# One dense column in four parts, tied between the four stages of the seam's inverse

## The chip, the cores and the metric

The kernel runs on one core of a Trainium2 chip. The metric is the device time of one execution in microseconds (us), as the median of several runs. It was 3087.81 us before the change (three runs, 3085.42 to 3102.24).

## The reference

Two layers act on 528 tokens (16 meta tokens and 512 others) of width 1024, in float32. Each layer is a half-step SwiGLU feed-forward block, a mixer, and a second feed-forward block, each closed by a layer norm. The mixer is what the change touches:

```python
def _mixer(x, w_in, ...):
    z = x @ w_in                                   # 1024 -> 7424 columns
    glu_a, glu_b, zr, gate_c, gate_r = split(z)
    yc = conv_branch(glu_a * sigmoid(glu_b))       # 31 taps per channel, layer norm, silu, matmul
    yr = rwkv_branch(zr)                           # 16 heads of 64; S is 64x64 for each head
    h = sigmoid(gate_c) * yc + sigmoid(gate_r) * yr
    return h @ w_out
...
def step(S, inp):                                  # the scan in rwkv_branch, token by token
    sa = einsum("bhvk,bhk->bhv", S, -kk_t)
    S = S * w_t + sa * (kk_t * a_t) + v_t * k_t
    return S, einsum("bhvk,bhk->bhv", S, r_t)
```

## The kernel before

Matrix products with weights are done in three float32r products (high by high, high by low part of the tokens, low by high part). A *dense column* is 128 columns of `w_in`: eight tiles of the inner dimension, three products each, in two halves of 264 tokens, 48 products in all (`mac`, L243). Its weights come by one transfer on SP's queue (`wunit`, L136), are split on ACT (`w_hi`, L145 or L147) and on DVE (`w_lo`, L158; for the gate columns 42 to 57 by an ACT copy and a subtracting transfer on POOL's queue, L151 and L152), and the sum is taken from PSUM by ACT or DVE. Two buffers each are there for the raw weights, for the split weights, and for the PSUM tile `mm` of a column.

The token-by-token scan is done in eight chunks of 64 tokens, for four groups `q` of four heads, one after the other. For each group:

- `prep` makes the decayed keys and queries from six dense columns (k, r and v for two pairs of heads).
- `scores` makes a first part for the meta tokens, and then for each chunk transposes (L1227) and score matrices (L1236). All of them use the one PSUM tile `sc`; ACT (L1229, L1241) and DVE (L1243, L1245) empty it before the next chunk may start. The triangular blocks go out to DRAM (`mscr`).
- `substitution` reads 16x16 blocks back (`im`), inverts them by 15 pairs of DVE steps (L1271, L1274), and brings the result through DRAM (`xdscr`) to the block diagonal `dd` by 16 transfers on SP's queue (L1285).
- `inverse` extends that to 64x64 blocks in four stages: 16 products (L1310), a masking by DVE (L1311), and three times 16 products (L1317) and an addition by DVE (L1318). ACT copies the result to `G`. It runs for two halves of the chunks: half 0 ahead of the scan, half 1 inside it.
- `meta` handles the meta tokens (L1336 to L1348 and `pairs`, L1426), and `scan` does the eight chunks: transposes (L1381), L1386, L1395 and L1398, L1403, with copies by ACT and updates of the state by DVE (L1409, L1410) between them.

The scan of group q carries the scores of group q+1 in its chunks. The *seam* is what stands in the program between two scans: the second substitution, the inverse of half 0 and `meta`. There are four inverses of half 0 in each layer: one ahead of the first scan and three at the seams between scans.

The remaining dense columns, for the convolution's input (`glu_b`, `glu_a`) and the gates (`gate`), are *fill*: a list from which `filler(n)` takes the next n. FILL0, FILL, FILLS and FILLP say how many are taken at which place. The convolution's 31 taps per block of channels are DVE work at low priority (L1065).

The order on each engine is not the program's order: a scheduler places instructions by priority (the place in the program, shifted by `high_priority`) as soon as its own estimates have their inputs and buffers ready. So it moves dense products of later columns up into places where PE would wait. Tiles of a pool take their buffers in the program's order. `nosync(later, earlier)` binds two instructions to an order and has no wait on the chip, where both are on one engine.

Of the kernel before, what the change touches and what calls it, by code (L numbers as in the profile page):

```python
# [10 lines left out]
AF = mybir.ActivationFunctionType  # L11
# [7 lines left out]
KT = D // P  # L19
SEQ = 512  # L20
NM = 16
T = NM + SEQ
# [46 lines left out]
TMP = 2  # L69


FILL0 = (0, 0, 0, 0, 2, 0, 0, 0, 2)
FILL = ((0, 0, 0, 0, 0, 0, 0, 0), (0, 0, 0, 0, 0, 0, 0, 0), (0, 0, 0, 0, 0, 0, 0, 0), (0, 1, 0, 1, 0, 1, 0, 0))
FILLS = (3, 3, 4, 2)
FILLP = ((0, 0, 0, 0, 0, 0), (0, 0, 0, 0, 0, 2), (0, 0, 0, 0, 0, 1), (0, 0, 0, 0, 0, 0))
LAST = 1
SCORES = (2, 1, 1, 1, 1, 1, 1, 1)
# [19 lines left out]
class Trunk:  # L97
# [72 lines left out]
    def stream(self, jobs, tail=0, before=None, ahead=None, between=None):  # L170


        def run(js):
            ws = [load() for load, mac, evac in js]
            if js is end and ahead is not None and AEARLY:
                ahead()
            for h in range(2):
                if h == 1 and js is end and between is not None:
                    if ahead is not None and not AEARLY:
                        ahead()  # L180
                    between()
                for w, (load, mac, evac) in zip(ws, js):
                    ps, products = mac(w, h)
                    self.together(products[:1])
                    self.together(products[1:])
                    evac(h, ps)

        end = jobs[len(jobs) - tail:]
        for job in jobs[:len(jobs) - tail]:
            run([job])  # L190
        if before is not None:
            before()
        run(end)
# [40 lines left out]
    def mac(self, pm, w, x, t0, n, nk, wk=0, xk=0, first=True, last=True):  # L234

        hi, lo = w
        xh, xl = x
        nc = self.nc
        for k in range(nk):
            for j, (a, b) in enumerate(((hi, xh), (hi, xl), (lo, xh))):  # L240
                for h in range(2):
                    s = t0 + h * n
                    m = self.issued = nc.tensor.matmul(  # L243
                        pm[:, h, :n], a[:, wk + k, :], b[:, xk + k, s:s + n],
                        start=first and k == 0 and j == 0,
                        stop=last and k == nk - 1 and j == 2)
                    if self.later is not None:
                        self.nosync(m, self.later)
                        self.later = None


    def setup(self):
# [199 lines left out]
    def ffn(self, l, which, t0, n, gname, bname, pre, final=False, head=None, extra=()):  # L452
# [197 lines left out]
        for f in range(m):  # L650
            gate(f, 0, ps[f], zs[f])
        for f, x in enumerate(heads(1)):
            gate(f, 1, x, zs[f])
# [115 lines left out]
    def mixer(self, l, last, pre, more):  # L769
        nc, tc = self.nc, self.tc  # L770
# [16 lines left out]
        first = [[pm[:, h, :T // 2] for h in range(2)] for pm in pms + [self.glu0]]  # L787
# [24 lines left out]
            self.cu.append(u)  # L812
        fill = []
        for ct in range(KT):
            fill += [lambda ct=ct: self.glu_b(ct), lambda ct=ct: self.glu_a(ct)]
        fill += [lambda o=o: self.gate(o) for o in range(2 * KT)]

        def filler(n):
            for _ in range(min(n, len(fill))):
                fill.pop(0)()  # L820

        self.mixer_begin(pms, filler)

        def prep(q):
            Q = {}
            for i, _ in enumerate(self.prep(q, Q)):
                filler(FILLP[q][i])
                self.taps(TAPP[q])
            return Q

        Q = prep(0)
        for c, _ in enumerate(self.scores(0, Q)):
            if c == 4:
                self.substitution(0, 0, Q)
            filler(FILL0[c])
            if c:
                self.taps(TAP0[2])
        self.substitution(0, 1, Q)
        self.inverse(0, 0, Q)
        self.meta(0, Q)  # L840
        N = prep(1)
        post = iter(())
        self.cuts = CUTS
        for q in range(4):
            scores = self.scores(q + 1, N) if q < 3 else iter(())
            early = None
            done = 0
            for c, _ in enumerate(self.scan(q, Q)):
                if c == 0:
                    self.inverse(q, 1, Q)  # L850
                with self.tc.high_priority(offset=-SC_LATE):
                    for _ in range(SCORES[c]):
                        next(scores, None)
                        done += 1
                        if done == 5 and q < 3:
                            self.substitution(q + 1, 0, N)
                if c >= POST:
                    next(post, None)
                if q == 3 and c >= G3:
                    if early is None:  # L860
                        early = self.post(q, Q)
                    with self.tc.high_priority(offset=-G3L):
                        next(early) if c < G3 + 5 else None
                filler(FILL[q][c])
                self.taps(TAP[q][c])
            for _ in post:
                pass
            if q < 3:
                self.substitution(q + 1, 1, N)
                self.inverse(q + 1, 0, N)  # L870
                self.meta(q + 1, N)
            post = early or self.post(q, Q)
            filler(FILLS[q])
            Q, N = N, prep(q + 2) if q < 2 else None
# [45 lines left out]
    def proj(self, col):  # L920
        w = self.loaded.pop(col) if col in self.loaded else self.load_in(col)
        pm = self.mm()
        self.mac(pm, w, self.x, 0, T // 2, KT)
        return pm

    def tv(self, x):
        return self.halves(x, 0, T // 2)
# [97 lines left out]
        nc.gpsimd.memset(self.dd, 0.0)  # L1025


    def glu_b(self, ct):
        self.glu_s = self.tmp("glus", 1)
        gv = self.tv(self.glu_s)  # L1030
        if ct == 0:
            self.nc.scalar.activation(gv, self.pv(self.glu0), AF.Tanh, scale=0.5)
        else:
            self.nc.scalar.activation(gv, self.pv(self.proj(8 + ct)), AF.Tanh, scale=0.5)

    def glu_a(self, ct):
        nc = self.nc
        pa = self.proj(ct)
        nc.vector.scalar_tensor_tensor(self.tv(self.glu_s), self.tv(self.glu_s), 1.0, self.pv(pa),
                                       op0=ALU.add, op1=ALU.mult)  # L1040
        nc.sync.dma_start(out=self.us[ct * P:(ct + 1) * P, :], in_=self.glu_s)
        self.convs.append(self.conv(ct))
# [27 lines left out]
                nc.sync.dma_start(out=self.cs[ct * P:(ct + 1) * P, a:], in_=acc[:, a:])  # L1070
            yield True

    def gate(self, o):

        pg = self.proj(50 + o if o < KT else 42 + o - KT)
        s = self.tmp("glus", 1)
        self.nc.scalar.activation(self.tv(s), self.pv(pg), AF.Tanh, scale=0.5)
        a = self.t0
        (self.nc.sync, self.nc.scalar, self.nc.gpsimd)[GQ].dma_start(out=self.gs[o * P:(o + 1) * P, a:], in_=s[:, a:])
# [211 lines left out]
            nc.sync.dma_start(out=xt0, in_=self.xs0[q].rearrange("s i t -> i s t"))  # L1291
            Q["xt0"] = xt0

    def inverse(self, q, g, Q):

        nc, mp = self.nc, self.mp
        N = NCH
        k = slice(g * N, (g + 1) * N)  # L1300
        U, d, dt = self.ut[:, k], self.dd[:, k, 0], self.dd[:, k, 1]
        t = mp.tile([P, NCH * 4, 32], F32, name="b4", bufs=B4).rearrange("p a b -> p (a b)")
        vt, y = (t[:, i * N * C:(i + 1) * N * C].rearrange("p (s i) -> p s i", i=C)
                 for i in range(2))
        ps = self.sc()[:, 0].rearrange("p (s t) -> p s t", t=C)

        halves = [slice(0, C), slice(C, P)]
        for i in range(N):
            for r in halves:
                nc.tensor.matmul(ps[r, i], U[r, i], d[r, i], start=True, stop=True)  # L1310
        nc.vector.tensor_tensor(vt, ps, self.mskb[:, None, :].to_broadcast([P, N, C]), op=ALU.mult)  # L1311
        x = dt
        for c0 in (0, 2 * NM, 2 * NM):
            cs = slice(c0, C)
            for i in range(N):
                for r in halves:
                    nc.tensor.matmul(ps[r, i, cs], vt[r, i], x[r, i, cs], start=True, stop=True)  # L1317
            nc.vector.tensor_tensor(y[:, :, cs], ps[:, :, cs], dt[:, :, cs], op=ALU.add)  # L1318
            x = y
        out = Q["G"].rearrange("a p e f t -> a (p e) f t")  # L1320
        out = out[0:C, :, 1, NM + g * 4 * C:NM + (g + 1) * 4 * C].rearrange(
            "a h (k e t) -> a k e h t", e=2, t=C)
        for e, r in enumerate(halves):
            nc.scalar.copy(out[:, :, e], y[r].rearrange("a (k h) t -> a k h t", h=4))


    def new_state(self):
# [400 lines left out]
```

## Time and profile before

| | |
|---|---|
| median of three runs | 3087.81 us |
| profiled execution | 3091.81 us |
| its span, first to last instruction | 3090.1 us |
| PE busy | 3007.7 us (97%) |
| DVE busy | 2278.4 us (74%) |
| ACT busy | 1435.9 us (46%) |
| mean granted TensorE clock | 0.981 |

The span lies within the execution's own time. Busy times of PE are modelled ends of pipelined matmuls. A row of the windows view has the window in us from the span's start, its length, the busy time and the count of instructions of each engine, the granted clock, the share of the DMA engines and GB/s; a mean clock of 0.82 is a mixture of stretches at 1.00 and at 0.50. A row of the timeline has start, duration, engine, line, operation, tiles, shape, count, and in brackets the idle time ahead and what ended it.

### The profile page before, as it was taken

How to read it: one execution, taken by the hardware profiler on the slowest of the kernel's cores; microseconds unless marked ns; L12 is line 12 of the kernel's file. 1: busy time of each engine (PE TensorE's matmuls, PEld its weight loads, DVE VectorE, ACT ScalarE, POOL GpSimd, SP SyncE). 2: the span in 40 equal slices, each digit the busy share in tenths (PEclk: the TensorE clock that was granted, in tenths of full speed). 3: DMA queues.
4: the chain of work that ended last, by engine and by line, in shares of the span. 5: the costliest groups of instructions: out<-in, count | busy, mean ns of one | idle time of the engine just before them, and what ended most of it. 6: DMA issues, size and time to landing. Idle time of an engine off the chain costs nothing.

```text
span 3090.1 us, 64229 instructions
## 1 busy us (share of the span) xinstructions
PE 3007.7 (97%) x26138; PEld 2883.1 (93%) x26138; DVE 2278.4 (74%) x4687; ACT 1435.9 (46%) x2551; POOL 178.5 (6%) x286
## 2 busy tenths in 40 slices
PE   8999999999999999999999999999999999999998
PEld 8999989888888899999999999899889889999998
DVE  5676777888886668666786768778788857677767
ACT  4454454344454444444454444543445545254443
POOL 0010000000000000010001000000000000001100
PEclk9999999899999999999999999999899999999999
DMA  6565534335355554565545654444254655546661
GB/s 180 144 148 130 127 116 150 94 90 136 95 135 137 170 145 123 135 148 142 127 128 127 151 130 120 136 134 105 73 137 111 151 131 167 154 121 146 151 145 57
DMA packets 555701, 405.29 MB, mean 131 GB/s; under 512 B 89292, under 2 KB 500288, under 8 KB 555406
## 3 DMA queue, kind: packets, MB, share of 16 engines
q1 hardware_dynamic: 519854, 308.49, 34.8%
q0 software_dynamic: 30944, 84.18, 14.8%
q10 hardware_dynamic: 4608, 8.52, 0.8%
q8 instruction: 205, 3.36, 0.5%
q14 instruction: 90, 0.74, 0.1%
HBM read 270.81 MB, written 47.12 MB: 103 GB/s over the span
## 4 chain that ended last, share of the span: by engine, by line
PE 80%; DVE 8%; DMA 5%; ACT 4%; issue 2%; SPq 1%; ACTq 0%; POOL 0%; DVEq 0%; POOLq 0%
PE mm L215 51%; PE mm L243 15%; PE ch L1403 2%; PE sc L1317 2%; PE tr L1386 1%; PE sc L1236 1%; PE ch L1395 1%; DMA w_raw<-in_w_in_dram 1%; DVE w_lo L158 1%; DVE cacc L1065 1%; DMA w_raw<-in_ffn_wu_dram 1%; ACT w_hi L147 1%; PE sc L989 1%; DVE ln_rstd L425 1%; DMA w_lo<-w_raw 1%
## 5 line engine op out<-in xcount | busy, mean ns | idle before, releaser
L215 PE MATMUL mm<-xh,w_hi 128*128 128x264 f32 (+1 forms) x1792 | 512.2, 287 | 11.3 <-ACT xh L441 5.9
L215 PE MATMUL mm<-xl,w_hi 128*128 128x264 f32 (+1 forms) x1792 | 511.1, 286 | 0.7 <-DVE xl L442 0.3
L215 PE MATMUL mm<-xh,w_lo 128*128 128x264 f32 (+1 forms) x1792 | 510.1, 285 | 0.5 <-DVE w_lo L158 0.5
L215 PE MATMUL mm<-hh,w_hi 128*128 128x264 f32 (+1 forms) x1408 | 399.3, 284 | 1.1 <-ACT hh L110 1.1
L215 PE MATMUL mm<-hl,w_hi 128*128 128x264 f32 (+1 forms) x1408 | 399.4, 284 | 0.5 <-DVE hl L111 0.4
L215 PE MATMUL mm<-hh,w_lo 128*128 128x264 f32 (+1 forms) x1408 | 399.6, 284 | 0.0
L243 PE MATMUL mm<-xh,w_lo 128*128 128x264 f32 x1760 | 387.9, 297 | 7.2 <-DMA w_lo<-w_raw 6.7
L243 PE MATMUL mm<-xh,w_hi 128*128 128x264 f32 x1760 | 384.0, 295 | 6.9 <-DVE kp L939 2.9
L243 PE MATMUL mm<-xl,w_hi 128*128 128x264 f32 x1760 | 383.6, 295 | 0.0
L1065 DVE SCALAR_TENSOR_TENSOR cacc<-cu,cw,cacc 128x528 f32<-128x528 f32 (+1 forms) x480 | 355.6, 752 | 4.2 <-ACT cacc L1063 0.4
L215 PEld LDWEIGHTS mm<-xh,w_hi 128*128 128x128 f32 x1792 | 339.3, 190 | 15.4 <-ACT xh L441 8.5
L215 PEld LDWEIGHTS mm<-xl,w_hi 128*128 128x128 f32 x1792 | 341.2, 190 | 2.4 <-DVE xl L442 2.3
L215 PEld LDWEIGHTS mm<-xh,w_lo 128*128 128x128 f32 x1792 | 340.9, 190 | 0.8 <-DVE w_lo L158 0.8
L120 ACT CAST w_hi<-sums 128x512 fp32r<-128x512 f32 (+1 forms) x204 | 154.7, 759 | 317.1 <-PE mm L215 205.4
L243 PEld LDWEIGHTS mm<-xh,w_lo 128*128 128x128 f32 x1760 | 283.2, 193 | 14.8 <-DMA w_lo<-w_raw 7.8
L243 PEld LDWEIGHTS mm<-xh,w_hi 128*128 128x128 f32 x1760 | 282.5, 193 | 13.4 <-DVE kp L939 3.2
L243 PEld LDWEIGHTS mm<-xl,w_hi 128*128 128x128 f32 x1760 | 282.1, 192 | 5.5
L215 PEld LDWEIGHTS mm<-hh,w_hi 128*128 128x128 f32 x1408 | 264.6, 188 | 1.8 <-ACT hh L110 1.5
L215 PEld LDWEIGHTS mm<-hl,w_hi 128*128 128x128 f32 x1408 | 264.9, 188 | 1.2 <-DVE hl L111 1.1
L215 PEld LDWEIGHTS mm<-hh,w_lo 128*128 128x128 f32 x1408 | 265.5, 189 | 0.1
L158 DVE TENSOR_TENSOR w_lo<-w_raw,w_hi 128x1024 fp32r<-128x1024 f32 (+1 forms) x192 | 204.0, 1064 | 74.7 <-ACT w_hi L147 68.3
L147 ACT CAST w_hi<-w_raw 128x1024 fp32r<-128x1024 f32 x136 | 142.4, 1049 | 249.8 <-PE mm L243 77.7
(362 smaller groups left out, 6838.4 us busy)
## 6 DMA issues: line engine op xcount, KB each, us to landing
w_raw<-in_w_in_dram SPq DMA_DIRECT2D x116, 512.0 KB
w_lo<-w_raw POOLq DMA_DIRECT2D x100, 512.0 KB, 5.0
w_raw<-in_ffn_wg_dram SPq DMA_DIRECT2D x88, 512.0 KB
w_raw<-in_ffn_wu_dram SPq DMA_DIRECT2D x88, 512.0 KB
w_raw<-in_ffn_wd_dram SPq DMA_DIRECT2D x80, 512.0 KB
w_lo<-w_raw POOLq DMA_DIRECT2D x68, 256.0 KB, 3.4
w_raw<-in_rwkv_wo_dram SPq DMA_DIRECT2D x16, 512.0 KB
w_raw<-in_conv_wo_dram SPq DMA_DIRECT2D x16, 512.0 KB
```

The lines of the kernel that those rows point to most:

```text
L120: self.nc.scalar.copy(hi, x)
L147: copy = self.nc.scalar.copy(hi[:, :kt], raw[:, :kt])
L158: sub = self.nc.vector.tensor_tensor(lo[:, k], raw[:, k], hi[:, k].bitcast(F32), op=ALU.subtract)
L215: self.issued = self.nc.tensor.matmul(pm, a[:, k, :], b[:, xk + k, s], start=first and k == 0 and j == 0, stop=last and k == nk - 1 and j ...
L243: m = self.issued = nc.tensor.matmul(pm[:, h, :n], a[:, wk + k, :], b[:, xk + k, s:s + n], start=first and k == 0 and j == 0, stop=last an ...
L425: nc.vector.reciprocal(rstd[:, :n], rstd[:, :n])
L989: nc.tensor.matmul(pm, w[a][r, o, :], x[b][r, s], start=j == 0, stop=j == 2)
L1065: tap = nc.vector.scalar_tensor_tensor(y, x, w, y, op0=ALU.mult, op1=ALU.add)
L1236: pairs.append(nc.tensor.matmul(ps[:, e, p * P:(p + 1) * P], FB[p][r, fs], G[r, p, 1, :, cs], start=True, stop=True))
L1317: nc.tensor.matmul(ps[r, i, cs], vt[r, i], x[r, i, cs], start=True, stop=True)
L1386: nc.tensor.matmul(tr[0:C, right(h)], G[:, h // 2, h % 2, 0, cs], sv[:, h, :], start=True, stop=True)
L1403: chain.append(nc.tensor.matmul(ch[rows, right(h)], SB[:, c, h, rows], va[:, h, :], start=False, stop=True, skip_group_check=True))
```

## The change

At each inverse of half 0 the next fill column is taken, its 48 products are cut in four parts of 12 (two tiles of the inner dimension), and one part is issued behind each of the four stages. `between` binds a part's first product behind the stage's last one, and the next stage's first product is bound behind the part's last (`after`; after the fourth part nothing is bound). The column's eviction (`column[1]`) follows the inverse. FILL0's last entry and three of the four entries of FILLS give up one column each, so each layer has the same columns as before. `glu_b`, `glu_a` and `gate` now get the PSUM tile handed in.

```diff
-FILL0 = (0, 0, 0, 0, 2, 0, 0, 0, 2)
+FILL0 = (0, 0, 0, 0, 2, 0, 0, 0, 1)
...
-FILLS = (3, 3, 4, 2)
+FILLS = (2, 2, 3, 2)
...
-        self.inverse(0, 0, Q)
+        self.inverse(0, 0, Q, fill.pop(0))
...
-                self.inverse(q + 1, 0, N)
+                self.inverse(q + 1, 0, N, fill.pop(0))
...
+    def parts(self, col, n):
+
+        w = self.loaded.pop(col) if col in self.loaded else self.load_in(col)
+        pm = self.mm()
+        for k in range(0, KT, n):
+            head = self.mac(pm, w, self.x, 0, T // 2, n, wk=k, xk=k, first=k == 0, last=k + n == KT)
+            yield pm, head, self.issued
...
-    def inverse(self, q, g, Q):
+    def inverse(self, q, g, Q, column=None):
...
+        parts = None if column is None else self.parts(column[0], KT // 4)
+        pm = after = None
+
+        def between(m):
+            nonlocal pm, after
+            if parts is not None:
+                pm, head, after = next(parts)
+                self.nosync(head, m)
...
-                nc.tensor.matmul(ps[r, i], U[r, i], d[r, i], start=True, stop=True)
+                m = nc.tensor.matmul(ps[r, i], U[r, i], d[r, i], start=True, stop=True)
+        between(m)
         nc.vector.tensor_tensor(vt, ps, self.mskb[:, None, :].to_broadcast([P, N, C]), op=ALU.mult)
...
-                    nc.tensor.matmul(ps[r, i, cs], vt[r, i], x[r, i, cs], start=True, stop=True)
+                    m = nc.tensor.matmul(ps[r, i, cs], vt[r, i], x[r, i, cs], start=True,
+                                         stop=True)
+                    if after is not None:
+                        self.nosync(m, after)
+                        after = None
+            between(m)
...
+        if pm is not None:
+            column[1](pm)
```

In the changed file the line numbers are higher: dense products are L244, the inverse L1328 and L1336, the scan's L1386 and L1403 are L1412 and L1429, the scores' L1227 and L1236 are L1237 and L1246.

The order on PE, in three places of layer 0. First, the end of the first scan's scores and the first stage of the seam's inverse. The tile `sc_7931` holds the last chunk's scores, `sc_8023` is the inverse's; a row of L243 is one or two dense products. Before:

```order
L1236 MATMUL sc_7931<-G_6769,FB_6771 128x128 x2
L1236 MATMUL sc_7931<-G_6769,FB_7024 128x128 x2
L243 MATMUL mm_8257<-xh_100,w_lo_8251 128x264
L243 MATMUL mm_8257<-xh_100,w_hi_8250 128x264 x2
...
L243 MATMUL mm_8390<-xl_101,w_hi_8383 128x264 x2
L243 MATMUL mm_8390<-xh_100,w_lo_8384 128x264 x2
L1381 MATMUL tr_8894<-ident_66,v_6955 64x128
L1381 MATMUL tr_8894<-ident_66,v_7208 64x128
L1310 MATMUL sc_8023<-dd_5617,ut_5615 64x64 x16
```

In the changed order the same place, from the scores of the chunk before the last on:

```order
L1246 MATMUL sc_7886<-G_6769,FB_7024 128x128 x2
L1237 MATMUL sc_7931<-ident_66,FB_6771 128x128
L1237 MATMUL sc_7931<-ident_66,FB_7024 128x128
L1246 MATMUL sc_7931<-G_6769,FB_6771 128x128 x2
L1246 MATMUL sc_7931<-G_6769,FB_7024 128x128 x2
L1328 MATMUL sc_8023<-dd_5617,ut_5615 64x64 x16
L244 MATMUL mm_8048<-xh_100,w_hi_8041 128x264 x2
```

The 127 dense products between the last scores and the inverse (the end of `mm_8257`, all of `mm_8321` and `mm_8390`) are no longer there; they stand behind the inverse, after the tied column `mm_8048`.

Second, a chunk of the same scan (`tr` and `ch` are the scan's PSUM tiles, `mm_8140` is a fill column). Before:

```order
L1403 MATMUL ch_7768<-va_7760,sb_5614 128x64 x4
L1236 MATMUL sc_7613<-G_6769,FB_6771 128x128 x2
L1236 MATMUL sc_7613<-G_6769,FB_7024 128x128 x2
L243 MATMUL mm_8140<-xh_100,w_lo_8134 128x264 x2
L243 MATMUL mm_8140<-xh_100,w_hi_8133 128x264 x2
L243 MATMUL mm_8140<-xl_101,w_hi_8133 128x264 x2
L1386 MATMUL tr_7808<-sv_7782,G_5619 64x64 x4
```

And now, one chunk of it:

```order
L1407 MATMUL tr_7756<-ident_66,v_6062 64x128
L1246 MATMUL sc_7565<-G_6769,FB_6771 128x128 x2
L1429 MATMUL ch_7643<-va_7635,sb_5614 128x64 x4
L1246 MATMUL sc_7565<-G_6769,FB_7024 128x128 x2
L1412 MATMUL tr_7756<-sv_7657,G_5619 64x64 x4
```

The dense rows are gone from it. Counted over the whole order, between the first product of a scan's own inverse (half 1) and the first product of the next seam's inverse (half 0), and from there to the next half 1:

| | layer 0, seam 1 | seam 2 | seam 3 | layer 1, seam 1 | seam 2 | seam 3 |
|---|---|---|---|---|---|---|
| dense products half 1 to half 0, before | 237 | 226 | 215 | 206 | 239 | 193 |
| now | 0 | 0 | 0 | 0 | 0 | 0 |
| half 0 of the group before to its half 1, before | 240 | 244 | 235 | 268 | 270 | 251 |
| now | 432 | 480 | 432 | 432 | 480 | 432 |

Ahead of the first inverse of a layer stand 195 (layer 0) and 168 (layer 1) dense products fewer than before. No product of a column that comes after the tied one in the program stands ahead of the tied column's first product at any of the eight inverses. Of the scheduler's reasons the order shows this much alone; the tied column's PSUM tile is one of the two `mm` buffers.

Third, the inverse's stages two to four at the same seam. Before:

```order
L1317 MATMUL sc_8023<-dd_5617,b4_8022 64x64 x15
L1348 MATMUL ch_8104<-small_5616,xt_7748 16x64 x4
...
L1317 MATMUL sc_8023<-b4_8022 64x32 x16
L1426 MATMUL ch_8121<-small_5616 16x64 x8
L243 MATMUL mm_8508<-xh_100,w_lo_8502 128x264
L1317 MATMUL sc_8023<-b4_8022 64x32 x16
```

Now:

```order
L1336 MATMUL sc_8023<-dd_5617,b4_8022 64x64 x15
L244 MATMUL mm_8048<-xh_100,w_hi_8041 128x264 x2
...
L244 MATMUL mm_8048<-xh_100,w_lo_8042 128x264 x2
L1336 MATMUL sc_8023<-b4_8022 64x32 x16
L244 MATMUL mm_8048<-xh_100,w_hi_8041 128x264 x2
...
L244 MATMUL mm_8048<-xh_100,w_lo_8042 128x264 x2
L1336 MATMUL sc_8023<-b4_8022 64x32 x16
L1374 MATMUL ch_8163<-small_5616,xt_7748 16x64 x4
```

Between the stages 12 products of the tied column stand now where a few products of other columns and `meta`'s small products stood; `meta` follows behind the inverse.

More of the change, by code (lines that the diff above doesn't have):

```diff
@@ L238, in mac @@
         nc = self.nc
+        head = None
         for k in range(nk):
@@ L246, in mac @@
                         stop=last and k == nk - 1 and j == 2)
+                    head = head or m
                     if self.later is not None:
@@ L249, in mac @@
                         self.later = None
+        return head
     def setup(self):
@@ L814, in mixer @@
         for ct in range(KT):
-            fill += [lambda ct=ct: self.glu_b(ct), lambda ct=ct: self.glu_a(ct)]
-        fill += [lambda o=o: self.gate(o) for o in range(2 * KT)]
+            fill += [(8 + ct if ct else None, lambda pm, ct=ct: self.glu_b(ct, pm)),
+                     (ct, lambda pm, ct=ct: self.glu_a(ct, pm))]
+        fill += [(50 + o if o < KT else 42 + o - KT, lambda pm, o=o: self.gate(o, pm))
+                 for o in range(2 * KT)]
         def filler(n):
             for _ in range(min(n, len(fill))):
-                fill.pop(0)()
+                col, use = fill.pop(0)
+                use(None if col is None else self.proj(col))
         self.mixer_begin(pms, filler)
@@ L1025, in mixer_begin, with glu_b, glu_a @@
         nc.gpsimd.memset(self.dd, 0.0)
-    def glu_b(self, ct):
+    def glu_b(self, ct, pm):
         self.glu_s = self.tmp("glus", 1)
         gv = self.tv(self.glu_s)
[L1031 to L1036, printed above, removed]
+        pm = self.glu0 if ct == 0 else pm
+        self.nc.scalar.activation(gv, self.pv(pm), AF.Tanh, scale=0.5)
+    def glu_a(self, ct, pa):
         nc = self.nc
-        pa = self.proj(ct)
         nc.vector.scalar_tensor_tensor(self.tv(self.glu_s), self.tv(self.glu_s), 1.0, self.pv(pa),
@@ L1071, in conv, with gate @@
             yield True
-    def gate(self, o):
-        pg = self.proj(50 + o if o < KT else 42 + o - KT)
+    def gate(self, o, pg):
         s = self.tmp("glus", 1)
```

## The prediction

> **What bounds the kernel.** I read the page's head first, then the two seam regions of the mixers, then each scan by itself, with all PE work and with the dense products alone.
>
> ```profile
> span 3090.1 us, 64229 instructions
> ...
> PE 3007.7 (97%) x26138; PEld 2883.1 (93%) x26138; DVE 2278.4 (74%) x4687; ACT 1435.9 (46%) x2551; POOL 178.5 (6%) x286
> ...
> PEclk9999999899999999999999999999899999999999
> ```
>
> TensorE bounds it: it lies idle for 82 of 3090 us. What the change can win is in the regions from the first to the last seam's inverse, one per layer (columns: window, its length, PE busy and count, then PEld, DVE, ACT, POOL, then the granted clock):
>
> ```profile
> 580.79:976.43 395.64, 379.36 (x3934) 343.72 (x3933) 311.79 (x805) 178.85 (x394) 13.91 (x33) 0.94 0.45 112
> 2119.60:2508.72 389.12, 375.61 (x3934) 340.83 (x3933) 307.78 (x772) 180.28 (x392) 14.79 (x34) 0.95 0.47 117
> ```
>
> Idle there is 16.3 + 13.5 = 29.8 us, and the clock gives away 6% of 395.6 and 5% of 389.1, 43 us: 73 us is the most that any new order could recover. The waits that the change's words speak of are small:
>
> ```profile
>   DVE b L1318: 1.5, 3
> ...
> PE sc L1310 <- DMA dd<-xdscr: 5.0, 6, 1.2
> PE mm L243 <- DMA w_lo<-w_raw: 6.7, 6, 2.1
> ```
>
> The first is PE's idle time ahead of the inverse's later stages until DVE has masked or added (1.5 us in all sixteen inverses), since other dense products already stand between them; the second is its wait for `dd` ahead of stage one.
>
> **The scans, where the order changes most.** The six stretches run from the first product of a scan's own inverse (half 1) to the first product of the next seam's inverse (half 0). First PE's whole work, then that of the dense products (L243) alone, where the bracket counts them:
>
> ```profile
> 636.48:705.57 69.09, 64.96 (x741) 1.00 0.34 88
> 760.22:823.59 63.37, 62.97 (x711) 1.00 0.44 113
> 876.11:941.79 65.68, 62.32 (x702) 1.00 0.59 147
> 2171.18:2246.30 75.12, 69.42 (x680) 0.82 0.30 74
> 2298.77:2364.78 66.01, 65.27 (x750) 1.00 0.45 115
> 2413.25:2475.05 61.80, 59.09 (x674) 1.00 0.62 153
> sum 401.07, PE 384.03; mean PE 64.00
> ```
>
> ```profile
> 636.48:705.57 69.09, 34.54 (x238) 30.13 (x237) 1.00 0.34 88
> 760.22:823.59 63.37, 33.93 (x226) 29.02 (x226) 1.00 0.44 113
> 876.11:941.79 65.68, 33.22 (x216) 27.70 (x215) 1.00 0.59 147
> 2171.18:2246.30 75.12, 30.77 (x207) 27.53 (x206) 0.82 0.30 74
> 2298.77:2364.78 66.01, 36.02 (x239) 30.82 (x239) 1.00 0.45 115
> 2413.25:2475.05 61.80, 30.77 (x194) 25.16 (x193) 1.00 0.62 153
> ```
>
> About 1316 dense products stand in them (the order's 237, 226, 215, 206, 239 and 193). In the changed order there are none. Their price is the pace of a dense run, here 16 products from the first row to the second; the two rows after these bound the wait at the end of the first stretch:
>
> ```profile
> 701.93 0.41 PE L243 MATMUL mm<-xh,w_hi 128*128 128x264 f32 x2
> ...
> 703.88 0.41 PE L243 MATMUL mm<-xh,w_lo 128*128 128x264 f32 x2
> ...
> 687.86 0.71 PE L1236 MATMUL sc<-G,FB 64*128 64x128 f32 x8
> ...
> 705.57 0.33 PE L1310 MATMUL sc<-dd,ut 64*64 64x64 f32 x2 [1.06 <-DMA dd<-xdscr]
> ```
>
> 1.95 us / 16 = 0.122 us, so 1316 products are 161 us. They now run behind the seam, after the products that stood there before. Whether that costs 161 us depends on how much shorter the stretches become. They are held by chains: a chunk of the scan passes from PE to ACT or DVE and back several times, a scores chunk waits for the one `sc` buffer, and after the last scores (688.6) the substitution and its transfers take until 705.6, 17 us, under 127 dense products.
>
> **What a chunk costs without fill.** At the full clock (window rows, then waits within), and in the one place where the kernel before already has next to no fill, the first scan of layer 1:
>
> ```profile
> 654.45:659.90 5.45, 4.42 (x52) 3.33 (x50) 5.17 (x10) 2.84 (x8) 0.00 (x0) 1.00 0.07 15
> 2189.09:2196.96 7.87, 6.68 (x45) 5.12 (x45) 4.67 (x9) 2.47 (x7) 0.00 (x0) 0.50 0.04 8
> 2181.60:2208.90 27.30, 24.29 (x152) 19.10 (x153) 16.43 (x31) 7.55 (x22) 0.00 (x0) 0.50 0.11 28
> ```
>
> ```profile
> 658.74 0.71 PE L1236 MATMUL sc<-G,FB 64*128 64x128 f32 x8 [0.46 <-ACT sb L1229]
> 659.90 0.68 PE L1386 MATMUL tr<-sv,G 128*64 128x64 f32 x8 [0.44 <-DVE sv L1410]
> ...
> 2189.09 1.08 PE L1386 MATMUL tr<-sv,G 128*64 128x64 f32 x8 [1.47 <-DVE sv L1410]
> 2196.96 1.09 PE L1386 MATMUL tr<-sv,G 128*64 128x64 f32 x8 [1.19 <-DVE sv L1410]
> ...
> 2218.59 0.68 PE L1386 MATMUL tr<-sv,G 128*64 128x64 f32 x8
> 2228.45 0.71 PE L1236 MATMUL sc<-G,FB 64*128 64x128 f32 x8
> ```
>
> 5.45 us warm, 7.87 us cold: after some 8 us without dense products the clock fell to 0.50 and stayed there for 27.3 us, until dense products came. In the changed order no scan has fill, so I take the cold value for all six; the warm one is the other end.
>
> The Trainium skill, "TensorE: Matmul & The Clock Gate", section "Why this matters for your kernels", says that the clock is kept as long as PE's gaps stay under about 3 us. By that rule every scan would stay warm. The rows speak against it: the longest gap in the cold chunks is 1.47 us.
>
> **The sum.**
> - Stretches. I take layer 1's first as the model. From its start (2171.2) to 2196.96 it is nearly unfilled: 25.8 us. Three more chunks at 7.87 bring the eighth: 23.6. From there to the end of the last scores it took 10.6 (2218.6 to 2229.2) with 34 dense products; less fill and a half clock offset each other: 10.6. The wait for `dd` was 17 us; the changed DVE order has almost nothing between the substitution's steps, so I take 13 (10 to 17). Together 73 us; six make 438 against 401: +37. With the 161 displaced: +198. Ends: warm chunks give 8 x 5.4 + 9 + 10 = 62 us, 372 in all, +132; 78 us each give +228.
> - The first seam of each layer. 195 and 168 dense products (24 + 20 us) stood between the fourth scores chunk and the inverse. The scores' evictions and the substitution remain in their place. In the rows below layer 0's stretch is 26.7 us, most of it dense; I estimate that it and its twin shorten by 5 us each: +34 (20 to 44).
>
> ```profile
> 554.08:580.79 26.71, 23.04 (x176) 21.70 (x175) 1.00 0.37 92
> ```
>
> - The inverse itself. Its four parts are the same products as the filler's that FILL0 and FILLS give up: no work is added. The 1.5 us ahead of L1317 go, and some cold stretches around the inverse: -10 (0 to -40). If this cover were gone instead, the stages would wait their DVE operation, under 1 us each.
> - The column's load, its two splits and its eviction move with it. On SP its load no longer stands between the substitution's transfers; PE waits for weights 6.7 us in all today. Behind the seam nine to ten columns now follow each other; those that subtract by DMA could wait up to 2.1 us each. I take 0 (up to +29 for 14 of them).
> - Taps: the order puts as many ahead of each inverse as before (140 and 140, 189 and 190), so DVE gets no new tail: 0.
>
> 198 + 34 - 10 = +222 us. The profiled execution took 3091.8 us, 4.0 above the median of 3087.8; from the median, 3310.
>
> **The rivals.**
> 1. The scans stay warm, as two chunks in layer 0 did: 132 + 34 - 10 = +156, so 3244. For it: 5.45 us at clock 1.00, with a single dense product in it. Against it: the chunks on both sides of it had fill, and 27.3 us in the second layer had almost none.
> 2. Cold, and the burst of columns behind the seam waits for weights, and the `dd` wait stays 17 us: 222 + 24 + 20 = +266, so 3354.
> 3. The other side: the change does what its words say and the displaced fill costs nothing, since the stretches shorten by all of it. Then half of the 73 us come back: 3051. It decides only if a stretch falls from 66.9 to below 40 us on average (161 + 34 us over six is 32 each); eight chunks at 5.4 alone are 43.
> 4. It doesn't do what it says in a way that matters: the order of the parts is real, but chains and fill balance, no change: 3088.
>
> **Chances.** The forecast 0.62, rival 1 0.22, rival 2 0.1, rival 3 0.03, rival 4 0.03. The forecast's own range is 3265 to 3345. From 3215 to 3370 the first three are held, leaving out some 0.1 to 0.2. A difference of 0.5%, 15 us, is what a measurement here can tell from none: faster 0.03, same 0.03, slower 0.94.
>
> **What would show it.** In the changed kernel: six scans with no dense product and PE idle or at clock 0.50; chunks near 7.9 us (warm: 5.4); a PE wait for `dd` of about 10 us or more at each of the eight seams where it was 1.2 at most; a granted clock well below 0.981; dense runs of 430 to 480 products between the inverses. I am wrong if the stretches fall to 45 us, or if dense products are found in the scans.

## The result and the profile after

The changed kernel takes 3312.76 us in the median (3312.13 to 3314.81), the one before beside it 3090.24: 1.0709 times as long (1.0686 to 1.0732).

The page of the changed kernel: span, busy times, and the granted clock in 40 slices.

```profile
span 3310.9 us, 64246 instructions
...
PE 3084.9 (93%) x26138; PEld 2936.5 (89%) x26138; DVE 2299.3 (69%) x4687; ACT 1438.4 (43%) x2551; POOL 178.2 (5%) x286
...
PEclk9999999979688999999999999989777789999999
```

PE executes as many instructions as before and is busy for 77 us more (3084.9 against 3007.7), and idle for 226 us instead of 82: 77 + 144 = 221 us, the whole loss. More busy time with the same work goes with the lower clock, 0.936 in the mean against 0.981. The row of the clock shows it in both mixers, and in no other place.

The six scan stretches, from a scan's own inverse to the seam's (PE alone, then the granted clock):

```profile
657.63:726.40 68.77, 46.52 (x499) 0.71 0.16 39
804.92:875.64 70.72, 51.07 (x509) 0.65 0.32 74
950.72:1017.67 66.95, 48.97 (x484) 0.62 0.33 82
2292.04:2359.70 67.66, 45.56 (x500) 0.72 0.16 39
2437.62:2515.85 78.23, 59.94 (x506) 0.57 0.27 67
2590.50:2662.34 71.84, 53.83 (x482) 0.58 0.31 75
sum 424.17, PE 305.89; mean PE 50.98
```

Before they took 401.07 us with 1316 dense products in them, at clock 1.00 in five of six. Now they take 424.17 us with none: 23 us longer, although 161 us of work have left them, and idle for 118 us.

Behind the first inverse of each layer and those of seams 1 and 2, up to the next half 1, the sums of six such rows, first of the changed kernel and then of the one before, whose 1508 dense products are now 2688:

```profile
sum 447.30, PE 439.51; mean PE 73.25
```

```profile
sum 315.38, PE 303.03; mean PE 50.51
```

That is 132 us more for 1180 more products (144 us at 0.122). The remaining 499 displaced products run after the third seam's inverse of each layer.

The waits of PE, longest in sum:

```profile
PE sc L1328 <- DMA dd<-xdscr: 79.6, 8, 10.7
PE tr L1412 <- DVE sv L1436: 14.5, 15, 1.7
PE sc L1246 <- ACT sb L1239: 11.5, 21, 1.1
```

The wait for `dd` ahead of the inverse was 5.0 us in all and is now 79.6, one of about 10 us at each of the eight inverses. It is the same transfer; the products that covered it are gone. The timeline at the first seam:

```profile
714.43 1.22 PE L1246 MATMUL sc<-G,FB 64*128 64x128 f32 x8 [0.46 <-ACT sb L1239]
726.40 1.91 PE L1328 MATMUL sc<-dd,ut 64*64 64x64 f32 x25 [10.74 <-DMA dd<-xdscr]
```

### The profile page after: what moved, and what is told of

It is laid out like the page before. It is cut to its first block, busy times and chain, and to the rows that moved or that the text cites. A ratio compares the mean times of both kernels' runs of the same rounds, so it can differ in the third digit from the quotient of the medians.

```text
span 3310.9 us, 64246 instructions
## 1 busy us (share of the span) xinstructions
PE 3084.9 (93%) x26138; PEld 2936.5 (89%) x26138; DVE 2299.3 (69%) x4687; ACT 1438.4 (43%) x2551; POOL 178.2 (5%) x286
## 4 chain that ended last, share of the span: by engine, by line
PE 75%; DVE 11%; DMA 6%; ACT 4%; issue 2%; SPq 2%; ACTq 0%; DVEq 0%
PE mm L215 47%; PE mm L244 13%; DVE cacc L1076 2%; PE ch L1429 2%; PE sc L1246 2%; PE sc L1336 2%; PE tr L1412 1%; PE ch L1421 1%; SPq L1295 1%; DMA w_raw<-in_ffn_wu_dram 1%; DVE w_lo L158 1%; DMA w_raw<-in_w_in_dram 1%; PE sc L1237 1%; DMA gscr<-glus 1%; DVE ln_rstd L428 1%
## 5 line engine op out<-in xcount | busy, mean ns | idle before, releaser
L244 PE MATMUL mm<-xh,w_hi 128*128 128x264 f32 x1760 | 378.2, 294 | 4.9 <-ACT w_hi L145 2.5
L244 PE MATMUL mm<-xh,w_lo 128*128 128x264 f32 x1760 | 371.3, 290 | 3.0 <-DMA w_lo<-w_raw 2.0
L244 PE MATMUL mm<-xl,w_hi 128*128 128x264 f32 x1760 | 369.1, 290 | 0.0
L244 PEld LDWEIGHTS mm<-xh,w_hi 128*128 128x128 f32 x1760 | 278.9, 191 | 11.9 <-ACT w_hi L145 2.9
L244 PEld LDWEIGHTS mm<-xh,w_lo 128*128 128x128 f32 x1760 | 277.7, 191 | 6.1 <-DMA w_lo<-w_raw 2.4
L244 PEld LDWEIGHTS mm<-xl,w_hi 128*128 128x128 f32 x1760 | 277.9, 191 | 2.4
```

Of the source, the lines that this page charges most:

```text
L244: m = self.issued = nc.tensor.matmul(pm[:, h, :n], a[:, wk + k, :], b[:, xk + k, s:s + n], start=first and k == 0 and j == 0, stop=last an ...
```

## The experiments

The theory that was tested: the tie that puts a part behind its stage holds the column's PSUM tile back, and with it every later column, so that the scans lose their fill ("held fill"). The first rival: the loss lies at the inverse, whose stages now wait for the parts. The second: the loss is the clock alone.

**Without the first tie.**

```diff
-                self.nosync(head, m)
```

> The changed kernel without the tie that puts a part behind its stage (the line nosync(head, m)); the tie that puts the next stage behind the part stays, as do the column's place in the program and its four parts. On PE 241, 232, 195, 240, 239 and 193 dense products stand in the six scan stretches again (0 in the changed kernel). Theory 'held fill' (the tied column keeps every later column from being drawn forward): the loss goes, 3080 to 3095 us. Rival 'inverse' (the loss lies at the inverse: its stages wait for the parts, meta comes later): most of it stays, since stages still wait for parts, over 3200. Rival 'place' (the column's place in the program costs): stays at 3313.

3107.65 us against 3095.35, ratio 1.0037 (1.0019 to 1.0055), a little above the expected band. One line makes 6.7 of the 7.1%. The parts now run ahead with the other fill (45 of the tied column's 48 products stand in the first scan), so this run does not try stages that wait for late parts.

**Without the second tie.**

```diff
-                    if after is not None:
-                        self.nosync(m, after)
-                        after = None
+                    after = None
```

> The changed kernel without the other tie: a stage no longer has to stand behind the part ahead of it; a part still stands behind its stage. The scan stretches still hold no dense product. 'Held fill': no gain, 3305 to 3320 us. 'Inverse': the stages are free of the parts, so a good share of the 222 us comes back, below 3250.

3316.18 us, ratio 1.0716 (1.0687 to 1.0744): nothing comes back. But the program is the same: with and without the second tie, every engine has the same instructions in the same order (64246 in both profiles). The scheduler's order obeys this tie anyway. So the tie costs nothing, and the run repeats the changed kernel; it does not test the first rival, although its expectation meant it to. What speaks against that rival is the trace: in the six stretches that begin with an inverse of half 0, summed above, PE is idle for 7.8 us (447.30 less 439.51), and before it was 12.4 (315.38 less 303.03).

**Without both ties.**

> The changed kernel without both ties: the column is issued in four parts inside the inverse, and nothing binds it. The order holds the same dense counts as without the first tie alone (241, 232, 195, 240, 239, 193 in the scans). 'Held fill': 3085 to 3100 us; if the second tie was what kept the run without the first one 0.4% above the kernel before, this one lies below it, at the kernel before. If the rest comes from the column's place in the program, it stays at +0.4%.

3108.17 us, ratio 1.004 (1.0023 to 1.0057). This program too is the same, instruction for instruction, as the one without the first tie alone (64235 in both profiles), and so is its time, again above the expected band. So the 0.4% don't come from the second tie. What is left of the change is the column's place in the program, with its four parts; which wait the 0.4% are was not settled. Half-clock windows lie at other places than before, some 24 us at the first seam of each layer (706 to 731 and 2246 to 2270 us).

**The first part free.**

```diff
-                pm, head, after = next(parts)
-                self.nosync(head, m)
+                free = pm is None
+                pm, head, after = next(parts)
+                if not free:
+                    self.nosync(head, m)
```

> The changed kernel with the first part alone freed from its stage; parts two to four stay tied. The scan stretches then hold 60, 60, 47, 60, 60 and 49 dense products: the first part (12) and one more column (48), as two PSUM buffers allow. 'Held fill': 336 products, 41 us, and 247 of the 363 that were missing ahead of the first inverses stay missing; the scans remain thinly filled, partly cold: 3200 to 3260 us. If the clock alone were the loss and a little fill held it, 3150 to 3200. 'Inverse': as the changed kernel, above 3290, since three of four parts are tied as before.

3248.47 us, ratio 1.0493 (1.0459 to 1.0527), inside the band of held fill. The count of 60 products in a stretch says how the holding works: with its first part free, the tied column takes one `mm` tile, one later column fits in the other, and the third stands behind the inverse, where the tied column is done. With the first part tied, not even the second tile is used. In the orders of this run, of the kernels before and after and of the run without the first tie, no `mm` tile has its first product ahead of that of a tile which the program takes earlier: the tied column's first product holds back all that follow. The split weights of the next column are not what it lacked: in the changed kernel's first scan (657.63 to 726.40 us) the last `w_hi` cast starts at 657.37 and the last `w_lo` at 663.25 us, and by the order both are for that column.

**Fill taken inside the scans.**

```diff
-FILL = ((0, 0, 0, 0, 0, 0, 0, 0), (0, 0, 0, 0, 0, 0, 0, 0), (0, 0, 0, 0, 0, 0, 0, 0), (0, 1, 0, 1, 0, 1, 0, 0))
-FILLS = (2, 2, 3, 2)
+FILL = ((0, 1, 0, 0, 0, 1, 0, 0), (0, 1, 0, 0, 0, 1, 0, 0), (0, 1, 0, 1, 0, 1, 0, 0), (0, 1, 0, 1, 0, 1, 0, 0))
+FILLS = (0, 0, 0, 2)
```

> The changed kernel with its ties, but the fill columns of FILLS are taken inside the scans (FILL gives two, two and three columns in scans 0 to 2, FILLS (0, 0, 0, 2)). 96, 96, 131, 96, 96 and 132 dense products stand in the scan stretches, nothing between the last scores and the inverse. 'Held fill': 647 products, 79 us, are hidden again and the scans are warmer, the wait for dd (80 us in all) stays: 3190 to 3235 us. 'Inverse': nothing at the inverse is changed, 3300 or more.

3164.42 us, ratio 1.0217 (1.0195 to 1.0239): 148 us come back with both ties in place, more than the expected 78 to 123. Its six stretches:

```profile
sum 385.95, PE 322.07; mean PE 53.68
```

They hold 647 products (79 us) and are still 38 us shorter than the unfilled ones. Fill is not only hidden; it also keeps the clock (0.86 to 0.95 in these stretches, against 0.57 to 0.72) and so shortens the small products. The expectation had put too little on that. The 79 and the 38 us make 117 of the 148; where the other 31 lie was not followed.

**Dummy products in the scans.**

```diff
+                if q < 3:
+                    with self.tc.high_priority(offset=-SC_LATE):
+                        self.issued = None
+                        self.keep(self.mm()[:, 0], 6)
+                        self.issued = None
                 filler(FILL[q][c])
```

> The changed kernel with six dummy products (128x512, of ones, into a PSUM tile that nobody reads) in every chunk of scans 0 to 2, 288 in all; they do no work for the output and stand in for fill. It parts the clock from the idle time. If the clock holds at 1.00 in the scans: chunks go from about 7.4 us back to 5.4 to 6, some 40 to 70 us come back, 3240 to 3275; the displaced 161 us stay lost. If the clock was the whole loss: below 3170. If six products a chunk don't hold it: 3313 to 3360, since they cost up to 0.22 us each at full clock.

3263.28 us, ratio 1.0534 (1.0505 to 1.0564): 288 products that do nothing, some 0.24 us apart in the trace, make the kernel 50 us faster. Its stretches:

```profile
651.91:716.38 64.47, 48.07 (x546) 0.89 0.17 41
794.31:858.05 63.74, 47.74 (x557) 0.93 0.34 83
934.14:991.72 57.58, 43.37 (x525) 0.91 0.36 92
2265.86:2329.70 63.84, 48.89 (x548) 0.90 0.17 41
2407.14:2476.56 69.42, 55.63 (x554) 0.78 0.31 77
2552.09:2616.41 64.32, 50.41 (x520) 0.79 0.33 81
sum 383.37, PE 294.11; mean PE 49.02
```

The clock is back at 0.78 to 0.93 and the stretches are 41 us shorter, with no dense product of a column in them. So at least 50 of the 218 us are the clock. The second rival, that it is all, falls: 169 us stay (3263.28 against 3094.6), and what the clock can still account for is an estimated 49 us, the difference of the mean clocks (0.966 here, 0.981 before) times the span of 3262.3.

**The first inverse of each layer alone, and the seams alone.**

```diff
-FILLS = (2, 2, 3, 2)
+FILLS = (3, 3, 4, 2)
...
-                self.inverse(q + 1, 0, N, fill.pop(0))
+                self.inverse(q + 1, 0, N)
```

> The changed kernel with the tied column at the first inverse of each layer alone; the three seams as before (FILLS (3, 3, 4, 2)). 195 and 168 dense products are missing ahead of those inverses, the scans hold 243, 225, 205, 227, 238 and 193. The prediction's term for them was +34 us (20 to 44): 3125. If the stretch doesn't shorten but grows, as the changed kernel's trace says of layer 0 (its inverse starts 5 us later with 24 us fewer done), +50 to +60: 3145.

3129.29 us, ratio 1.0093 (1.0057 to 1.0129), +35 us: the prediction's term. The larger figure in this expectation rested on a misreading. The changed kernel's profile is late from the first feed-forward block on (see the end), so a first inverse that starts 5 us later does not mean that the stretch ahead of it grew.

```diff
-FILL0 = (0, 0, 0, 0, 2, 0, 0, 0, 1)
+FILL0 = (0, 0, 0, 0, 2, 0, 0, 0, 2)
...
-        self.inverse(0, 0, Q, fill.pop(0))
+        self.inverse(0, 0, Q)
```

> The other half: the tied column at the three seams alone, the first inverse as before (FILL0 ends with 2). The scans hold no dense product. If the terms add up: 222 less the first inverses' 34, about 3280 us; with 55 for them about 3260.

3300.06 us, ratio 1.0656 (1.0622 to 1.0689), +205 us, above both sums of the expectation. 35 + 205 are 240 where both together cost 218: the halves overlap by some 20 us, little more than the intervals allow (18 to 40 for the one, 192 to 213 for the other). That the three seams make most of the loss is shown; where the overlap lies is not.

**Seams tied, fill in the scans, first inverses as before.** The two edits above together.

> Fill columns taken inside the scans as in the run with FILL in scans 0 to 2 (647 products there, now 640), ties at the three seams, but the first inverse of each layer as in the kernel before. That run lies 69 us above the kernel before; 35 us of that are what the first inverses alone cost. 'Held fill', with terms that add: 3125 to 3140 us, the rest being the wait for dd at six seams (about 10 us each, uncovered) less the cold clock that the seams had before. If the seams with fill in the scans cost nothing more: 3095 to 3110.

3148.08 us, ratio 1.0172 (1.0137 to 1.0208), outside the expected band: only 16 of the 35 us come back. The wait that stays is the seams'; a sixth one, the second row, is put down to a tap on DVE that ended last:

```profile
PE sc L1328 <- DMA dd<-xdscr: 39.0, 5, 14.6
PE sc L1328 <- DVE cacc L1076: 9.8, 1, 9.8
```

The six stretches show where a part of the rest went: with 640 products in them they are 15.5 us longer than in the run with fill in the scans (401.46 against 385.95), at a clock of 0.75 to 0.89 where it was 0.86 to 0.95. Why the clock fell there is not settled.

```profile
sum 401.46, PE 330.45; mean PE 55.08
```

**Two versions without the tied column.** From the kernel before, with fill columns moved from FILLS into the scans:

```diff
-FILL = ((0, 0, 0, 0, 0, 0, 0, 0), ...
-FILLS = (3, 3, 4, 2)
+FILL = ((1, 0, 0, 0, 0, 0, 0, 0), ...
+FILLS = (2, 3, 4, 2)
```

> The kernel before, without any of the change, with one fill column of FILLS's first entry taken in chunk 0 of the first scan instead (FILL[0] begins with 1, FILLS (2, 3, 4, 2)). In layer 1 the chunks of that scan that held 0, 0 and 0 dense products hold 58, 14 and 15. The 27.3 us at half clock there are worth up to 14 us, and 5 to 6 us of idle: if fill in a scan is what counts, 3075 to 3085 against 3090 to 3095, 10 to 18 us faster. If that place was hidden by something else: no change.

3092.43 us against 3096.81, ratio 0.9987 (0.9966 to 1.0008): no change that can be told. The first scan of layer 1 did become what was wanted:

```profile
2172.85:2239.72 66.87, 66.60 (x736) 1.00 0.36 91
```

75.12 us at 0.82 became 66.87 at 1.00, with 56 products more in it. All six stretches together take 400.58 us (401.07 before) and hold 1423 products, 107 more, some 13 us of work that is hidden there now. The six stretches behind the inverses lose it again: they hold 1390 products, 118 fewer (14 us), and take as long as before (315.38), at a clock of 0.83 to 0.93 where it was 0.85 to 1.00:

```profile
sum 314.01, PE 301.40; mean PE 50.23
```

```diff
-FILL = ((0, 0, 0, 0, 0, 0, 0, 0), (0, 0, 0, 0, 0, 0, 0, 0), (0, 0, 0, 0, 0, 0, 0, 0), ...
-FILLS = (3, 3, 4, 2)
+FILL = ((0, 1, 0, 1, 0, 0, 0, 0), (0, 1, 0, 1, 0, 0, 0, 0), (0, 1, 0, 1, 0, 0, 0, 0), ...
+FILLS = (1, 1, 2, 2)
```

> The kernel before with two fill columns of FILLS taken in chunks 1 and 3 of each of the scans 0 to 2 (FILLS (1, 1, 2, 2)). Layer 1's first scan holds 53, 15 and 24 products in the chunks that had 0. The counts of the stretches are 285, 217, 198, 257, 221 and 176 (237, 226, 215, 206, 239 and 193 before): the first scans gain, the others lose a few. 'Held fill' gives the gain of layer 1's first scan, 10 to 18 us, less up to 5 us for the others: 3075 to 3090.

3079.72 us against 3096.81, ratio 0.9944 (0.9923 to 0.9964): 17 us faster than the kernel before, and the only version here that is clearly faster than it. Its stretches:

```profile
sum 390.84, PE 381.39; mean PE 63.56
```

They are 10 us shorter than before (401.07) and hold 1354 products, 38 more: 9.5 us of idle instead of 17. That accounts for the 17 us in part only: this profiled execution was the slowest of its twelve runs (3091.56 us), as long as that of the kernel before (3091.81).

## Why the prediction was right

The forecast was 3310 us and +222; measured were 3312.76 and +222.5 (the profiled executions differ by 220.8 in their spans). Its mechanism is shown: the one tie removes the fill from the scans, and without it all but 0.4% of the loss is gone.

- **The scan stretches, +198.** They measured 161 + 23 = 184: 424 us where the model said 438. A cold chunk is indeed near 7.9 us, and the dense products are all gone, but the scans are not cold throughout: with the two levels 1.00 and 0.50, a clock of 0.57 to 0.72 is half clock for 56 to 86% of a stretch. The six lie between the warm end (372) and the cold value. The run with dummy products comes near the warm end: 383 us at a clock of 0.78 to 0.93.
- **The first inverses, +34.** From the fourth chunk's scores on, layer 0 took 30.3 us to its first inverse and takes 26.9 now, with PE busy for 8.6 of them; the rows are of the kernel before and of the changed one. (The prediction's row for this, from 554.08 on, began with the fifth chunk's scores; the fourth's stand at 550.48.)

```profile
550.46:580.79 30.33, 30.06 (x254) 1.00 0.34 83
```

```profile
559.23:586.14 26.91, 8.60 (x61) 0.59 0.21 42
```

  Layer 1 went from 27.5 to 26.8 us. So 4 of the 44 us are saved where 10 were assumed, and the term is 40; alone it measured 35 (18 to 40).
- **The inverse itself, -10.** The displaced 205 us of products (1679 in all) cost 194 us where they now stand (132 us in the six stretches behind the inverses, and 62 us between the third seam's inverse of each layer and the next layer norm's first product): -11. In the six stretches the clock is 0.96 to 0.97, against 0.85 to 1.00 before, so a part of the seams' cold windows did go, as assumed.
- **Weights, 0.** PE waits for the subtracting transfers of `w_lo` 2.0 us in all, less than the 6.7 before: the burst of nine to ten columns does not starve.
- **Taps, 0.** DVE's busy time is 2299 us against 2278, and no wait for a tap stands among PE's longer ones.
- **The wait for `dd`.** "About 10 us or more at each of the eight": 79.6 us in eight. The estimate of 13 us for the end of a stretch was near: 715.65 to 726.40 is 10.7.

The terms' errors were -14, +6 and -1, and the two profiles differ by 9 us before the change's first place is reached: the nearly exact sum is partly luck. The range, 3215 to 3370, is the better measure of what was known.

The rule of the Trainium skill ("TensorE: Matmul & The Clock Gate", "Why this matters for your kernels") that gaps under about 3 us keep the clock does not hold for these scans. In the changed kernel no wait of PE in the six stretches, up to the wait for `dd` at their end, is longer than 1.7 us, and the clock is at a half for most of the scans. The rival that keeps the scans warm (3244) was wrong for the change as it stands. Dense products between the small ones restored the clock, real or dummy. They shortened the gaps as well (the waits for the state are 0.7 us at most with the dummies), so which of the two counts was not separated.

## What to carry to other kernels

A tie can cost everything that queues behind the tied instruction's buffer, not only the instruction: before binding work into a slot, count in the order what else can still be drawn forward past it. A tie that the order obeys anyway costs nothing, and a run without it tests nothing, like the second tie here: compare the two orders first. Buffers that are handed out in the program's order make a late first use a barrier for all later users; here 1679 products were held by one line. Fill belongs where the chain waits longest (here the scans and the wait for `dd`), not where it is easiest to place.

## What the runs showed of the hardware that was not expected

- Six dummy products in each chunk, about 1.4 us of work in a chunk of 4.7 to 7.6 us in the first scan, raised the granted clock of the six stretches: it was between 0.57 and 0.72, and is between 0.78 and 0.93. They paid for themselves: 50 us less for 288 products. In the first stretch half clock is left only from about 700 us on, at the end with the wait for `dd`.
- An unfilled scan is not cold from end to end: in the changed kernel's first scan two chunks take 7.9 and 6.8 us and then, without a single dense product, 6.0 and 4.7 us, with the small products at their full speed again (0.65 us for the eight of L1412 where it was 1.1):

```profile
678.70 1.11 PE L1412 MATMUL tr<-sv,G 128*64 128x64 f32 x8 [0.69 <-DVE sv L1436]
686.61 1.09 PE L1412 MATMUL tr<-sv,G 128*64 128x64 f32 x8 [1.20 <-DVE sv L1436]
693.45 0.99 PE L1412 MATMUL tr<-sv,G 128*64 128x64 f32 x8 [1.52 <-DVE sv L1436]
699.43 0.65 PE L1412 MATMUL tr<-sv,G 128*64 128x64 f32 x8 [0.71 <-DVE sv L1436]
704.15 0.65 PE L1412 MATMUL tr<-sv,G 128*64 128x64 f32 x8 [0.70 <-DVE sv L1436]
```

- The first feed-forward block, the same in all thirteen profiles, differs by up to 9 us between executions: its last products start between 418.9 and 427.5 us, and the first score matrix of the first group between 539.6 and 548.6, at 539.83 in the profile before and at 548.59 in the one after.
